# Hybrid diffusion trunk: differential attention first beside the other projections, softmax division of A and B at the output, out-projection in two halves of four k-tiles

## Chip, core and metric

One core of a Trainium2 chip runs the whole inference step, two layers. The metric is the device time of the kernel in microseconds; smaller is better. TensorE (PE) does the matmuls, VectorE (DVE), ScalarE (ACT) and GpSimd (POOL) the rest, and SyncE (SP) and POOL issue the transfers. Each engine takes its instructions from a queue in a fixed order.

## What is computed

There are 128 context tokens and 1024 latent tokens of width 1024, and 256 cached tokens. Each of the two layers is

```python
h = adaln(x, g_attn, shift, scale)                    # modulated RMSNorm
qa, ka, va, qb, kb, vb, qc, kc, vc = split_qkv(h, w_in)   # one projection, 18 blocks of 128 columns
oa = neighborhood_attn(qa, ka, va, cache, rpb)        # A: 4 heads x 64, keys near in the 2-D grid + cached ones, bias
ob = window_attn(qb, kb, vb, cache, sink)             # B: 8 q heads, 2 kv heads, window 128, sink
oc = diff_attn(qc, kc, vc, lam, subln_g)              # C: 4 heads, softmax1 - lam * softmax2 over all keys
x = x + gate * (concat(oa, ob, oc) @ w_out)
h = adaln(x, g_ffn, ...)
x = x + gate * conv_ffn(h)                            # 1024 -> 2 x 2816 -> 1024, width-3 convolution between
```

Every q and k head is RMS-normalised (B and C with a rotary embedding). A softmax row is `exp(s - max) / sum`; in B the sum also holds the sink. The new keys and values of the context tokens are outputs too.

## The kernel before

The tokens lie along the free axis, 1156 columns with padding, in three chunks of some 386. A product of two f32 matrices is three matmuls in fp32r on high and low parts (`gemm`, L480), so that a projection block (`inproj`, L491) is three chunks of 24 matmuls. A block of q or k goes on, for each chunk: ACT squares and copies it out of PSUM, PE sums over the head with a matmul by ones (L515), `rsqrt` follows with Ln and Exp on ACT (L433, L434), one step on DVE (L435) and one on POOL (L436); then POOL scales (L517), DVE finishes (L518), for B and C the rotary embedding runs on DVE and POOL (L525 to L528), and ACT and POOL write the high and low parts `hl` (L551, L552), which SP stores to DRAM as `d`. An attention head loads them again as q and k on POOL's queue (`loadq64` L597, `loadk64` L607; L674 and L678 for C). V, the bias, the caches and the weights come by SP's queue.

An attention block computes scores (L657, L706 for C), DVE adds mask or bias and takes the row's maximum, ACT takes Exp with the row's sum (L660), DVE divides (L853 for A, L797 for B; for C POOL at L715 and DVE at L716 combine the two softmaxes), and `tpv` (L633) transposes P on PE, four tiles to a PSUM bank of the two `tb` banks (L643), ACT copies a bank to `pt` (L645), and PE multiplies by V (L648). After each bank of transposes comes its PV.

The order within a layer is that of the string PLAN (L52), whose steps are projection blocks (`A:4+2`), attention heads (`a:0`, `b:0` for a kv head with two pairs of q heads) and the opening and closing of pools (`fA`, `xA`):

```python
PLAN = "A:4+2 A:0 A:5+3 A:1 mF fA a:0 a:1 a:2 a:3 xA B:11 B:10 B:6 B:7 fB b:0 B:8 B:9 b:1 xB C:16 C:17 C:14 C:15 C:12 C:13"
```

This is program order. A list scheduler then places the instructions into the queues by what is ready in its own model of time, earlier code first; so A attention runs beside the projections that stand behind it, B attention beside C's projections, and C attention (`attnC`, L662) beside `outproj_ab` (L272), the six k-tiles of the out-projection whose heads are A and B, with the O of these read back from DRAM (`odr`). In layer 0 six pieces of the next modulation (`mod_piece`) lie there too. The last two k-tiles (C's) come with the residual and the norm of the FFN. A pool that is opened where another was closed gets its memory, and what is loaded there waits for the last readers.

Of the kernel before, what the change touches and what calls it, by code (L numbers as in the profile page):

```python
# [1078 lines left out]
```

## Time and profile before

| | us |
|---|---|
| median of three runs | 3502.01 (3489.72 to 3503.1) |
| the profiled execution | 3498.61 |
| its span, first to last instruction | 3496.8 |
| PE busy | 3313.9 (95%) |
| DVE busy | 2205.8 (63%) |
| ACT busy | 1524.2 (44%) |
| POOL busy | 1024.6 (29%) |
| mean granted clock of PE, share of full speed | 0.974 |

A layer is some 1000 us of norm, projections, attention and out-projection, in layer 0 from 0 to 1000 and in layer 1 from 1775 to 2700, and some 700 to 800 us of FFN behind it, in which PE is never idle. In layer 0, A attention lies at 150 to 350, B attention at 350 to 605, C attention at 605 to 885. A page's busy time is the sum over the span; the windows of a stage say more of that stage. The granted clock is given as a share of 2.4 GHz.

### The profile page before, as it was taken

The numbers are of one execution on the slowest core, as the hardware profiler recorded it, in microseconds if no ns is written. First come the engines' busy times: TensorE is split into PE (matmuls) and PEld (weight loads), VectorE is DVE, ScalarE is ACT, GpSimd is POOL, SyncE is SP. The second block draws the span as 40 slices with busy tenths as digits, with TensorE's granted clock in tenths as the row PEclk, the third lists the DMA queues.
The fourth block names the chain that finished last, engine by engine and source line by source line (L and its number), as shares of the span: only waits on it lengthen the run. The fifth ranks groups of instructions, "written<-read, shape, count | busy, mean of one in ns | idle before, by whom it ended". The sixth has DMA issues, their size and how long they took to land. (4 is left out here: it accounts for less than half of the span.)

```text
span 3496.8 us, 53582 instructions
## 1 busy us (share of the span) xinstructions
PE 3313.9 (95%) x20014; PEld 2985.7 (85%) x20014; DVE 2205.8 (63%) x5070; ACT 1524.2 (44%) x2941; POOL 1024.6 (29%) x1034
## 2 busy tenths in 40 slices
PE   6989998998899999999999999989888999999999
PEld 4967875865799999999989788768667999999999
DVE  5356677676775875687473557787867544544445
ACT  4555666556522222222245556666664322232222
POOL 5444252432711011101164443423335110111110
PEclk9999998998999999999999999989989999999999
DMA  5765554562122322222137654633401111111112
GB/s 198 204 157 146 129 129 156 139 188 54 40 65 62 91 83 64 72 91 77 43 128 192 168 149 120 142 115 106 102 17 37 34 44 44 43 37 46 46 39 95
DMA packets 197300, 340.23 MB, mean 97 GB/s; under 512 B 59408, under 2 KB 134816, under 8 KB 196656
## 3 DMA queue, kind: packets, MB, share of 16 engines
q1 hardware_dynamic: 183376, 288.89, 27.0%
q0 software_dynamic: 13664, 47.91, 6.7%
q8 instruction: 159, 2.61, 0.3%
q14 instruction: 101, 0.83, 0.1%
HBM read 282.20 MB, written 58.73 MB: 97 GB/s over the span
## 5 line engine op out<-in xcount | busy, mean ns | idle before, releaser
L488 PE MATMUL mm<-h,whl 128*128 128x386 f32 (+2 forms) x4512 | 882.3, 345 | 11.0 <-DVE t L435 4.5
L488 PEld LDWEIGHTS mm<-h,whl 128*128 128x128 f32 x4512 | 802.5, 190 | 29.2 <-DVE t L435 6.4
L488 PE MATMUL s<-h,whl 128*128 128x386 f32 (+2 forms) x4128 | 781.4, 343 | 19.2 <-ACT h L475 9.3
L488 PEld LDWEIGHTS s<-h,whl 128*128 128x128 f32 x4128 | 737.9, 190 | 35.7 <-ACT h L475 14.0
L370 POOL TENSOR_TENSOR whl<-wraw,whl 128x1024 fp32r<-128x1024 f32 (+1 forms) x96 | 227.1, 2367 | 1347.0 <-ACT whl L369 1260.9
L369 ACT ACTIVATE whl<-wraw 128x1024 fp32r<-128x1024 f32 (+1 forms) x246 | 234.9, 957 | 480.5 <-PE s L488 264.7
L660 ACT ACTIVATE P<-P,nm 128x641 f32<-128x641 f32 (+4 forms) x360 | 345.0, 959 | 131.5 <-DVE nm L708 44.3
L488 PE MATMUL s<-ah,whl 128*128 128x384 f32 (+1 forms) x1272 | 356.5, 341 | 2.7 <-DVE x L870 2.6
L643 PE MATMUL tb<-ident,P 128*128 128x128 f32 x1600 | 285.8, 295 | 17.6 <-DVE P L716 12.6
L645 ACT ACTIVATE pt<-tb 128x512 f32<-128x512 f32 (+2 forms) x456 | 235.9, 541 | 152.4 <-PE tb L643 150.7
L648 PE MATMUL pv<-pt,v 128*64 128x128 f32 x3200 | 272.6, 291 | 23.3 <-ACT pt L645 22.0
L648 PEld LDWEIGHTS pv<-pt,v 128*64 128x64 f32 x3200 | 173.1, 139 | 121.8 <-ACT pt L645 52.0
L643 PEld LDWEIGHTS tb<-ident,P 128*128 128x128 f32 x1600 | 189.0, 146 | 98.4 <-issue 63.4
L870 DVE SCALAR_TENSOR_TENSOR x<-s,m,x 128x257 f32<-128x257 f32 (+3 forms) x347 | 169.8, 514 | 145.7 <-PE s L488 145.4
L488 PE MATMUL mm<-ah,whl 128*128 128x384 f32 (+1 forms) x840 | 243.2, 341 | 0.4 <-DVE x L870 0.3
L488 PEld LDWEIGHTS s<-ah,whl 128*128 128x128 f32 x1272 | 234.3, 189 | 7.0 <-PE mm L488 2.8
L657 PE MATMUL s<-k,q 128*128 128x256 f32 (+2 forms) x816 | 184.5, 339 | 36.4 <-DMA q<-d 16.2
L488 PE MATMUL mm<-o,whl 128*128 128x384 f32 (+1 forms) x984 | 211.6, 353 | 5.0 <-ACT o L628 1.7
L488 PE MATMUL s<-al,whl 128*128 128x384 f32 (+1 forms) x636 | 215.8, 339 | 0.0
L870 DVE SCALAR_TENSOR_TENSOR x<-mm,m,x 128x257 f32<-128x257 f32 (+3 forms) x293 | 144.1, 514 | 113.5 <-PE mm L488 113.1
L370 DVE TENSOR_TENSOR whl<-wraw,whl 128x768 fp32r<-128x768 f32 (+1 forms) x150 | 166.4, 1110 | 46.7 <-ACT whl L369 46.1
L488 PEld LDWEIGHTS mm<-o,whl 128*128 128x128 f32 x984 | 179.3, 196 | 15.1 <-ACT whl L369 3.5
(195 smaller groups left out, 4942.0 us busy)
## 6 DMA issues: line engine op xcount, KB each, us to landing
wraw<-wup SPq DMA_DIRECT2D x88, 512.0 KB
mraw<-wmod SPq DMA_DIRECT2D x48, 512.0 KB
mraw<-wmv SPq DMA_DIRECT2D x96, 256.0 KB
wraw<-wdn SPq DMA_DIRECT2D x64, 384.0 KB
k<-d POOLq DMA_DIRECT2D x80, 288.5 KB, 6.8
wraw<-win SPq DMA_DIRECT2D x36, 512.0 KB
wraw<-woab SPq DMA_DIRECT2D x48, 384.0 KB
rope<-rope SPq DMA_DIRECT2D x36, 386.0 KB
```

What stands on the lines that cost most here:

```text
L369: nc.scalar.activation(hl[:, 0, :n], raw[:, :n], AF.Copy)
L370: lo_eng.tensor_tensor(hl[:, 1, :n], raw[:, :n], hl[:, 0, :n].bitcast(F32), op=ALU.subtract)
L488: nc.tensor.matmul(ps, w_, r_[:, a:b], start=(i == 0), stop=(i == tot - 1))
L643: nc.tensor.transpose(t[:, 128 * j:128 * j + 128], it[0], self.ident)
L645: nc.scalar.activation(pt[:, :n], t[:, :n], AF.Copy)
L648: nc.tensor.matmul(ps[64 * i:64 * i + 64, :128], V[:, vb], pt[:, 128 * j:128 * j + 128], start=first[i], stop=left[i] == 0)
L657: nc.tensor.matmul(dst, q, view(ks[i]), start=(i == 0), stop=(i == 1))
L660: self.nc.scalar.activation(P[:, :n], P[:, :n], AF.Exp, scale=-1.0, bias=nm, accum_out=sums)
L870: nc.vector.scalar_tensor_tensor(xx, ps[:, s - a:e - a], m[:, col + ob, v:v + 1], xx, op0=ALU.mult, op1=ALU.add)
```

## The change

PLAN begins with C: its blocks 14, 12, 16, then heads 0 and 1, the other C blocks, heads 2 and 3, with all A and B blocks behind them in program order. After that come A attention in a pool of its own, B attention with the out-projection of A's and C's four k-tiles (`outproj_first`) behind it, and the four k-tiles of B, whose O stays in SBUF, with the residual and norm. Weights of the out-projection are loaded once for t = 0 and once for t = 1 and 2 together. For the latent blocks of A and B, `softrow` writes the row's sum into a column of `sums`; after each half of the blocks a reciprocal is taken, PE turns the columns into rows (`rows_over`), and one DVE instruction multiplies 512 columns of O by them. `tpv` first writes all transposes and copies, then all PV. The sink copy moves from DVE to POOL, and buffer counts change. Lines of the kernel after are 10 to 40 higher: L488 is L498, L515 is L525, L517 is L527, L436 is L446, L526 is L536, L552 is L562, L597 is L607, L607 is L617, L643 is L651, L648 is L660, L657 is L681, L706 is L730.

```diff
-PLAN = "A:4+2 A:0 A:5+3 A:1 mF fA a:0 a:1 a:2 a:3 xA B:11 B:10 B:6 B:7 fB b:0 B:8 B:9 b:1 xB C:16 C:17 C:14 C:15 C:12 C:13"
+PLAN = "C:14+12 C:16 fC c:0 c:1 C:15+13 C:17 c:2 c:3 mF A:4+2 A:0 A:5+3 A:1 B:11 B:10 B:6 B:7 mP B:8 B:9 xC"
 QY = {"A": "p", "B": "p", "C": "p"}
 NM0, NMC = 8, 3
 MODF = (3, 4)
-NT_I, NQG_I, NHL_I, NR_I = 7, 5, 3, 2
-NQ_A, NK_A, NV_A, NB_A, NP_A, NT_A = 2, 2, 2, 7, 3, 3
-NQ_B, NK_B, NV_B, NP_B, NT_B = 3, 2, 1, 5, 4
-NQ_C, NK_C, NV_C, NP_C, NT_C = 2, 3, 1, 7, 3
+NT_I, NQG_I, NHL_I, NR_I = 6, 5, 2, 2
+NQ_A, NK_A, NV_A, NB_A, NP_A, NT_A = 2, 4, 2, 7, 5, 6
+NQ_B, NK_B, NV_B, NP_B, NT_B = 3, 2, 1, 6, 6
+NQ_C, NK_C, NV_C, NP_C, NT_C = 2, 2, 1, 5, 5
...
-OT = {"A": 0, "B": 2, "C": 6}
-INORDER = ["C", "B", "A"]
+OT = {"A": 0, "C": 2, "B": 4}
...
-                self.odr = self.dram.tile([6, 128, W], F32, name=f"odr{l}")
+                self.odr = self.dram.tile([4, 128, W], F32, name=f"odr{l}")
...
                     elif step[0] == "f":
-                        ap, aps = self.open(step[1], "right")
+                        cp, cs = self.open(step[1], "right")
                     elif step[0] == "x":
-                        aps.close()
-                    elif step[0] == "a":
-                        self.attnA(ap, int(step[2:]))
-                    elif step[0] == "b":
-                        self.attnB(ap, int(step[2:]))
+                        cs.close()
+                    elif step[0] == "c":
+                        self.attnC(cp, int(step[2:]))
...
-                cp, cs = self.open("C")
-                self.attnC(cp)
                 xp, xs = self.open("x", "right")
                 x = xp.tile([128, KT, XW], F32, name="x")
                 for t in range(3):
                     self.loadx(x, t)
+                obp, obs = self.open("OB")
+                self.mmtags = TAGS["F"]
+                ap, aps = self.open("A", "right")
+                for h in range(4):
+                    self.attnA(ap, h)
+                aps.close()
                 ab, abs_ = self.open("oab")
                 if l == 0:
                     for j in (4, 5):
                         self.mod_piece(l, j, ab, self.mm(), NMC)
-                self.outproj_ab(x, ab)
+                ap, aps = self.open("B", "right")
+                self.op = obp
+                for kv in range(2):
+                    self.attnB(ap, kv)
+                aps.close()
+                self.outproj_first(x, ab)
...
-                ow = [self.finO(ohp, t, {k: self.O[k][:, OCHUNK[t][0]:OCHUNK[t][1]] for k in (6, 7)}, 12) for t in range(3)]
+                ow = [self.finO(ohp, t, {k: self.O[k][:, OCHUNK[t][0]:OCHUNK[t][1]] for k in range(4, 8)}, 24) for t in range(3)]
                 for ts in ((0,), (1, 2)):
                     for ob in range(KT):
-                        if ob % 4 == 0:
-                            whl = self.wload(a["woc"][l, ob // 4], nc.vector)
+                        if ob % 2 == 0:
+                            whl = self.wload(a["wo"][l, 1, ob // 2], nc.vector)
                         for t in ts:
                             c0, c1 = OCHUNK[t]
                             ps = self.mm()
-                            self.gemm(ps[:, :c1 - c0], whl, (6, 7), (2 * (ob % 4), 2 * (ob % 4) + 1), ow[t], 0, c1 - c0)
+                            self.gemm(ps[:, :c1 - c0], whl, range(4, 8), [4 * (ob % 2) + i for i in range(4)], ow[t], 0, c1 - c0)
...
-    def outproj_ab(self, x, pool):
+    def outproj_first(self, x, pool):
         nc, a, l = self.nc, self.a, self.l
-        for t in range(3):
-            c0, c1 = OCHUNK[t]
-            n = c1 - c0
-            raw = pool.tile([128, 6, 388], F32, name="oraw", bufs=1)
-            nc.sync.dma_start(raw[:, :, :n], self.odr[:, :, c0:c1].rearrange("k p w -> p k w"))
-            ow = self.finO(pool, t, {k: raw[:, k, :n] for k in range(6)}, 14)
+        for ts in ((0,), (1, 2)):
+            ow = {}
+            for t in ts:
+                c0, c1 = OCHUNK[t]
+                raw = pool.tile([128, 4, 388], F32, name="oraw", bufs=1)
+                nc.sync.dma_start(raw[:, :, :c1 - c0], self.odr[:, :, c0:c1].rearrange("k p w -> p k w"))
+                ow[t] = self.finO(pool, t, {k: raw[:, k, :c1 - c0] for k in range(4)}, 16)
             for ob in range(KT):
-                whl = self.wload(a["woab"][l, ob], nc.vector if (t, ob) > (0, 3) else nc.gpsimd)
-                ps = self.mm()
-                self.gemm(ps[:, :n], whl, range(6), None, ow, 0, n)
-                self.addx(x, ob, ps, c0, c1, 16)
+                if ob % 2 == 0:
+                    whl = self.wload(a["wo"][l, 0, ob // 2], nc.vector)
+                for t in ts:
+                    c0, c1 = OCHUNK[t]
+                    ps = self.mm()
+                    self.gemm(ps[:, :c1 - c0], whl, range(4), [4 * (ob % 2) + i for i in range(4)], ow[t], 0, c1 - c0)
...
-        O = self.op.tile([128, W], F32, name="O", bufs=2)
+        O = self.op.tile([128, W], F32, name="O", bufs=2 if kt < 4 else 4)
...
-        ps = self.bank("pv")
-        left = [sum(it[2] == i for it in items) for i in range(2)]
-        first = [True, True]
+        pts = []
         for g in range(0, len(items), 4):
             its = items[g:g + 4]
             n = 128 * len(its)
@@ -643,14 +651,30 @@
                 nc.tensor.transpose(t[:, 128 * j:128 * j + 128], it[0], self.ident)
             pt = ap.tile([128, 512], F32, name="pt", bufs=bufs)
             nc.scalar.activation(pt[:, :n], t[:, :n], AF.Copy)
-            for j, (_, vb, i) in enumerate(its):
-                left[i] -= 1
-                nc.tensor.matmul(ps[64 * i:64 * i + 64, :128], V[:, vb], pt[:, 128 * j:128 * j + 128],
-                                 start=first[i], stop=left[i] == 0)
-                first[i] = False
+            pts.append(pt)
+        ps = self.bank("pv")
+        left = [sum(it[2] == i for it in items) for i in range(2)]
+        first = [True, True]
+        for g, (_, vb, i) in enumerate(items):
+            left[i] -= 1
+            nc.tensor.matmul(ps[64 * i:64 * i + 64, :128], V[:, vb], pts[g // 4][:, 128 * (g % 4):128 * (g % 4) + 128],
+                             start=first[i], stop=left[i] == 0)
+            first[i] = False
         for dst, p0, p1, view in outs:
             nc.scalar.activation(dst, view(ps[p0:p1, :128]), AF.Copy)
 
+    def rows_over(self, r, n):
+
+        t = self.tb()
+        for u in range(4):
+            o = t[:, 128 * u:128 * u + 128]
+            if n == 1:
+                self.nc.tensor.transpose(o, bcast(r[:, u:u + 1], [[0, 128]]), self.ident)
+            else:
+                for i in range(2):
+                    self.nc.tensor.matmul(o[64 * i:64 * i + 64], bcast(r[:, u, i:i + 1], [[0, 64]]), self.ident, start=True, stop=True)
+        return t
...
-                        nc.vector.tensor_copy(P[:, n:n + 1], sk)
+                        nc.gpsimd.tensor_copy(P[:, n:n + 1], sk)
...
-                        self.softrow(P, n + 1, last, ss)
-                        nc.vector.reciprocal(ss, ss)
-                        nc.vector.tensor_scalar(P[:, :n], P[:, :n], ss, None, op0=ALU.mult)
+                        if qb is None:
+                            self.softrow(P, n + 1, last, ss)
+                            nc.vector.reciprocal(ss, ss)
+                            nc.vector.tensor_scalar(P[:, :n], P[:, :n], ss, None, op0=ALU.mult)
+                        else:
+                            self.softrow(P, n + 1, last, sums[:, qb, i:i + 1])
                         Ps.append(P)
                     qo = C0 if qb is None else L0 + 128 * qb
                     self.tpv(ap, [(Ps[i][:, 128 * k:128 * k + 128], kb, i) for k, kb in enumerate(kbs) for i in range(2)], V, NT_B,
                              [(O[:, qo:qo + 128], 0, 128, lambda z: z)])
-                nc.sync.dma_start(self.odr[OT["B"] + h0 // 2], O)
+                    if qb in (3, 7):
+                        half = sums[:, qb - 3:qb + 1]
+                        nc.vector.reciprocal(half, half)
+                        R = self.rows_over(half, 2)
+                        oo = O[:, L0 + 512 * (qb // 4):L0 + 512 * (qb // 4) + 512]
+                        nc.vector.tensor_tensor(oo, oo, R, op=ALU.mult)
...
-                    self.softrow(P, n, nm[:, 1:2], ss)
-                    nc.vector.reciprocal(ss, ss)
-                    nc.vector.tensor_scalar(P[:, :n], P[:, :n], ss, None, op0=ALU.mult)
+                    if cb is None:
+                        self.softrow(P, n, nm[:, 1:2], ss)
...
+                if cb % 2 == 1:
+                    half = sums[:, 2 * cb - 2:2 * cb + 2]
+                    nc.vector.reciprocal(half, half)
+                    R = self.rows_over(half, 1)[rows]
+                    oo = O[rows, L0:L0 + T].rearrange("p (r b c) -> p b r c", r=ROWS, c=16)[:, cb - 1:cb + 1]
+                    nc.vector.tensor_tensor(oo, oo, R.rearrange("p (b r c) -> p b r c", b=2, c=16), op=ALU.mult)
```

How this moves instructions, at three places of layer 0. In each row the count of equal instructions stands at the end. First, PE's queue at the start of A attention, where L488 (after: L498) are projection matmuls, L515 (L525) the ones-matmul of a chunk, L657 (L681) scores, L643 transposes of P. Before:

```order
L488 MATMUL s<-h,whl 128x384 x22
L488 MATMUL s<-h,whl 128x386 x9
L515 MATMUL mm<-t,ones_86 128x386
L488 MATMUL s<-h,whl 128x386 x13
L657 MATMUL s<-k,q 128x128 x2
L488 MATMUL mm<-h,whl 128x386 x19
L515 MATMUL s<-t,ones_86 128x384
L488 MATMUL mm<-h,whl 128x386
L657 MATMUL s<-k,q 128x384 x2
```

and after:

```order
L525 MATMUL mm<-t,ones_86 128x386
L498 MATMUL mm<-h,whl 128x384 x29
L525 MATMUL s<-t,ones_86 128x386
L498 MATMUL s<-h,whl 128x386 x24
L525 MATMUL mm<-t,ones_86 128x384
L525 MATMUL s<-t,ones_86 128x386 x2
L525 MATMUL mm<-t,ones_86 128x384
L525 MATMUL s<-t,ones_86 128x386
L681 MATMUL s<-k,q 128x128
L681 MATMUL s<-k,q 128x384
L681 MATMUL s<-k,q 128x256 x2
```

The scores of A's first head stood between projection matmuls; now they stand behind the last of them, with five ones-matmuls in a row ahead.

Second, POOL's queue at the same place; d_0 is A's q of block 0, d_2 its k. Before:

```order
L517 TENSOR_TENSOR qg<-qg,t 128x386
L436 TENSOR_TENSOR t<-t 128x386
L547 TENSOR_TENSOR hl<-qg,hl 128x6x4x16 x2
L517 TENSOR_TENSOR qg<-qg,t 128x386
L436 TENSOR_TENSOR t<-t 128x386
L597 DMA q<-d_0_800 64x1152 x4
L552 TENSOR_TENSOR hl<-qg,hl 128x386
L517 TENSOR_TENSOR qg<-qg,t 128x384
L436 TENSOR_TENSOR t<-t 128x384
```

and after, the end of B's last block and the first loads of A:

```order
L527 TENSOR_TENSOR qg<-qg,t 128x384
L446 TENSOR_TENSOR t<-t 128x384
L536 TENSOR_TENSOR t<-t,rope 128x384
L562 TENSOR_TENSOR hl<-qg,hl 128x384
L527 TENSOR_TENSOR qg<-qg,t 128x386
L446 TENSOR_TENSOR t<-t 128x386
L536 TENSOR_TENSOR t<-t,rope 128x386
L562 TENSOR_TENSOR hl<-qg,hl 128x386
L607 DMA q<-d_0_3757 64x1152 x2
L617 DMA k<-d_2_3553 64x1154 x4
L607 DMA q<-d_0_3757 64x1152 x2
L617 DMA k<-d_2_3553 64x1154 x4
```

The loads of A's q and k stood between POOL's work on chunks; now they stand behind the last chunk's.

Third, PE's queue at the start of C attention, where L706 (after: L730) are scores and L586 turns the context's V. Before:

```order
L643 MATMUL tb<-ident,P 128x128 x4
L657 MATMUL s<-k,q 128x256 x2
L706 MATMUL s<-k,q 128x128 x2
L643 MATMUL tb<-ident,P 128x128 x2
L648 MATMUL pv<-pt,v 64x128 x8
L643 MATMUL tb<-ident,P 128x128 x4
L706 MATMUL s<-k,q 128x512 x2
L648 MATMUL pv<-pt,v 64x128 x2
L643 MATMUL tb<-ident,P 128x128 x4
```

and after:

```order
L498 MATMUL s<-h,whl 128x386 x22
L525 MATMUL tb<-t,ones_88 128x386
L498 MATMUL mm<-h,whl 128x386 x24
L525 MATMUL tb<-t,ones_88 128x386
L586 MATMUL pv<-ident,qg 128x128 x3
L586 MATMUL mm<-ident,qg 128x128 x3
L586 MATMUL s<-ident,qg 128x128 x3
L730 MATMUL s<-k,q 128x128 x2
L730 MATMUL s<-k,q 128x512 x4
L730 MATMUL s<-k,q 128x256 x2
L730 MATMUL s<-k,q 128x512 x2
```

The first scores of C stood between B's scores, transposes and PV; now they stand behind the ones-matmul of C's last q chunk and the nine transposes of V, with no other work between.

## Rows read from the trace of the kernel before

**Rows 1.** The page's first part: busy us of each engine, share, instructions.

```profile
PE 3313.9 (95%) x20014; PEld 2985.7 (85%) x20014; DVE 2205.8 (63%) x5070; ACT 1524.2 (44%) x2941; POOL 1024.6 (29%) x1034
```

**Rows 2.** Windows: stretch, length, busy PE PEld DVE ACT POOL (instructions), clock, DMA, GB/s.

```profile
175.00:350.00 175.00, 157.55 (x1036) 130.68 (x1035) 100.20 (x279) 98.02 (x229) 80.18 (x100) 0.98 0.58 152
350.00:490.00 140.00, 136.19 (x990) 118.64 (x989) 96.35 (x318) 87.06 (x205) 54.28 (x61) 0.99 0.50 129
490.00:605.00 115.00, 101.68 (x755) 70.82 (x757) 91.84 (x344) 79.79 (x183) 31.07 (x53) 0.90 0.52 148
605.00:750.00 145.00, 141.68 (x928) 117.96 (x928) 107.15 (x245) 82.61 (x145) 64.59 (x67) 0.98 0.53 141
750.00:885.00 135.00, 115.24 (x740) 70.35 (x740) 89.24 (x246) 81.46 (x150) 36.21 (x37) 0.87 0.36 109
...
1200.00:1300.00 100.00, 100.00 (x571) 100.00 (x570) 63.40 (x123) 23.44 (x36) 14.36 (x6) 1.00 0.23 71
...
1890.00:2085.00 195.00, 183.15 (x1192) 156.75 (x1191) 118.23 (x317) 114.46 (x266) 86.53 (x102) 0.97 0.56 150
2085.00:2225.00 140.00, 136.81 (x999) 120.55 (x998) 93.25 (x303) 84.86 (x198) 55.69 (x70) 1.00 0.54 137
2225.00:2365.00 140.00, 121.41 (x907) 86.88 (x905) 107.39 (x388) 96.24 (x218) 51.49 (x75) 0.92 0.50 132
2365.00:2490.00 125.00, 117.28 (x743) 100.72 (x744) 102.73 (x235) 74.12 (x130) 46.28 (x47) 0.94 0.41 109
2490.00:2600.00 110.00, 88.77 (x611) 61.97 (x610) 82.04 (x215) 72.83 (x133) 33.01 (x34) 0.88 0.14 35
```

**Rows 3.** Waits of PE in 175 to 300: total us, times, longest.

```profile
PE s L657 <- DMA k<-d: 8.1, 4, 4.2
...
PE tb L643 <- DVE P L853: 0.6, 1, 0.6
```

**Rows 4.** Waits of PE in 500 to 590.

```profile
PE s L657 <- DMA q<-d: 7.7, 1, 7.7
```

**Rows 5.** Windows: C's last head alone, layer 0.

```profile
807.00:863.00 56.00, 44.60 (x294) 30.08 (x294) 47.44 (x129) 36.95 (x65) 13.16 (x11) 0.82 0.07 13
```

**Rows 6.** Costliest groups: PV matmuls; behind the bars idle before, by releaser.

```profile
L648 PE MATMUL pv<-pt,v 128*64 128x128 f32 x3200 | 272.6, 291 | 23.3 <-ACT pt L645 22.0
```

**Rows 7.** Groups by shape, DVE: the division, B and A; total us, mean ns.

```profile
L797 DVE TENSOR_SCALAR P<-P,ss 128x640 f32<-128x640 f32 x96 | 60.8, 635 | 1.3
...
L853 DVE TENSOR_SCALAR P<-P,ss 128x640 f32<-128x640 f32 x64 | 47.1, 738 | 1.2
```

**Rows 8.** Timeline of PE: start, us for all, instruction, count.

```profile
522.64 0.89 PE L643 MATMUL tb<-ident,P 128*128 128x128 f32 x6
523.63 1.15 PE L648 MATMUL pv<-pt,v 128*64 128x128 f32 x16
```

**Rows 9.** Groups by shape, POOL: rsqrt's last step; loads of q, issue.

```profile
L436 POOL TENSOR_TENSOR t<-t 128x386 f32<-128x386 f32 x52 | 54.4, 1046 | 4.5 <-DVE t L435 4.4
...
L597 POOL DMA_DIRECT2D q<-d x48 | 25.5, 542 | 9.9 <-DMA k<-d 5.3 <-PE s L657 4.1 <-DMA d<-hl 0.5
```

**Rows 10.** Groups by shape, DVE: a step of the rotary embedding.

```profile
L525 DVE STREAM_SHUFFLE t<-qg 128x386 f32<-128x386 f32 x36 | 21.4, 593 | 0.0
```

**Rows 11.** Groups by shape, ACT: a step of rsqrt.

```profile
L434 ACT ACTIVATE t<-t 128x386 f32<-128x386 f32 x52 | 27.4, 526 | 0.9
```

**Rows 12.** Timeline of POOL: A's last context k part, then the load waiting for it.

```profile
108.46 0.46 POOL L533 TENSOR_TENSOR hl<-qg,hl 128x128 fp32r<-128x128 f32 x1 [1.97 <-ACT hl L532]
115.22 2.13 POOL L607 DMA_DIRECT2D k<-d  x4 [6.30 <-issue]
```

**Rows 13.** DMA issues: KB each, median us from issue to landing.

```profile
k<-d POOLq DMA_DIRECT2D x80, 288.5 KB, 6.8
...
q<-d POOLq DMA_DIRECT2D x64, 144.5 KB, 5.6
```

**Rows 14.** Timeline of PE where A attention begins, layer 0.

```profile
146.80 1.04 PE L488 MATMUL s<-h,whl 128*128 128x386 f32 x5
147.68 0.33 PE L657 MATMUL s<-k,q 128*128 128x128 f32 x2
```

**Rows 15.** Instructions of line L716: duration ns min/median/max.

```profile
L716 DVE SCALAR_TENSOR_TENSOR P<-P,ss x72: 331/1548/2614, 568.8 to 2580.2; 128x1280 f32<-128x1280 f32 x64, 128x128 f32<-128x128 f32 x8
```

More of the change, by code (lines that the diff above doesn't have):

```diff
@@ L187, in run @@
                             gens = [g for g in gens if next(g, None) is not None]
-                        if step[0] != "A":
+                        if step[0] != "C":
                             self.gate = None
@@ L208, in run @@
                 abs_.close()
-                cs.close()
                 self.mmtags = MM_SOLO
@@ L229, in run @@
                 ohs.close()
+                obs.close()
                 os_.close()
@@ L270, in run @@
             xs.close()
[L272 removed]
+    def outproj_first(self, x, pool):
         nc, a, l = self.nc, self.a, self.l
[L274 to L284 removed]
+        for ts in ((0,), (1, 2)):
[5 more added lines that the diff above has]
+                ow[t] = self.finO(pool, t, {k: raw[:, k, :c1 - c0] for k in range(4)}, 16)
+            for ob in range(KT):
+                if ob % 2 == 0:
[4 more added lines that the diff above has]
+                    self.gemm(ps[:, :c1 - c0], whl, range(4), [4 * (ob % 2) + i for i in range(4)], ow[t], 0, c1 - c0)
+                    self.addx(x, ob, ps, c0, c1, 16)
     def loadx(self, x, t):
@@ L660, in softrow, with attnC @@
         self.nc.scalar.activation(P[:, :n], P[:, :n], AF.Exp, scale=-1.0, bias=nm, accum_out=sums)
-    def attnC(self, ap):
+    def attnC(self, ap, h):
         nc, l = self.nc, self.l
@@ L665, in attnC @@
         lam = self.lam[l]
-        O = V = None
-        for h in range(4):
+        if True:
             blk, rw = h // 2, 64 * (h % 2)
@@ L689, in attnC @@
             if h % 2 == 0:
-                O = self.newO(OT["C"] + h // 2)
+                self.OC = self.newO(OT["C"] + h // 2)
+            O = self.OC
             rows = slice(rw, rw + 64)
@@ L733, in attnC @@
                                 self.subln(ap, O, c0, c1)
+            if h % 2 == 1:
+                nc.sync.dma_start(self.odr[OT["C"] + h // 2], O)
     def subln(self, ap, O, c0, c1):
@@ L761, in attnB @@
                 O = self.newO(OT["B"] + h0 // 2)
+                sums = ap.tile([128, 8, 2], F32, name="sums", bufs=2)
                 for qb in [None] + list(range(8)):
@@ L823, in attnA @@
             rows = slice(64 * (h % 2), 64 * (h % 2) + 64)
+            sums = ap.tile([128, 8], F32, name="sums", bufs=2)
             for cb in [None, 0, 1, 2, 3]:
@@ L850, in attnA @@
                                                        op0=ALU.add, op1=ALU.min, accum_out=nm[:, 1:2])
-                    self.softrow(P, n, nm[:, 1:2], ss)
-                    nc.vector.reciprocal(ss, ss)
-                    nc.vector.tensor_scalar(P[:, :n], P[:, :n], ss, None, op0=ALU.mult)
+                    if cb is None:
+                        self.softrow(P, n, nm[:, 1:2], ss)
+                        nc.vector.reciprocal(ss, ss)
+                        nc.vector.tensor_scalar(P[:, :n], P[:, :n], ss, None, op0=ALU.mult)
+                    else:
+                        self.softrow(P, n, nm[:, 1:2], sums[:, 2 * cb + rg:2 * cb + rg + 1])
                     Ps.append(P)
@@ L1010, in prep @@
     o["win"] = wblocks(f["w_in"], 18).reshape(DEPTH, 18, 128, 1024)
-    wo = wblocks(f["w_out"], 8)
-    o["woab"] = wo[:, :, :, :6].reshape(DEPTH, 8, 128, 768)
-    o["woc"] = wo[:, :, :, 6:].reshape(DEPTH, 2, 4, 128, 256).transpose(0, 1, 3, 2, 4).reshape(DEPTH, 2, 128, 1024)
+    wo = f["w_out"].reshape(DEPTH, 8, 128, 4, 2, 128)[:, [0, 1, 6, 7, 2, 3, 4, 5]].reshape(DEPTH, 2, 4, 128, 4, 2, 128)
+    o["wo"] = wo.transpose(0, 1, 4, 3, 5, 2, 6).reshape(DEPTH, 2, 4, 128, 1024)
     up = wblocks(f["w_up"], 44).reshape(DEPTH, 2, FB, 128, 1024)
```

## Prediction

> **What bounds the kernel now.** I read the page's totals first [rows 1]: PE 3313.9 of 3496.8 us, 95%, DVE 63%, ACT 44%, POOL 29%. By busy time the kernel is a TensorE kernel, so an edit pays only where it shortens PE's own work or PE's waiting. The profiled run took 3498.6 us, 1.8 us more than its span and 3.4 us less than the median of 3502.01; the sum is made against 3498.6 and the 3.4 us are put back at the end.
>
> The Trainium skill, Perfetto Trace Analysis, section Identifying the Most-Contended Engine, says that matmul busy time is a poor measure of how near TensorE is to its limit, and to use weight-load busy. Here weight loads are at 85%, ten points lower [rows 1]; by that reading there is more to win than the 95% says. The sum does not use it.
>
> Second, the stage windows [rows 2]. The dense stretch 1200 to 1300 is the yardstick: PE 100.00 of 100, 571 matmuls, 0.175 us each, granted clock 1.00 (2.4 GHz). For other stretches I call *lost* the length less PE busy times granted clock. Layer 0's attention: 20.6 us (175 to 350, A attention beside projections), 5.2 (350 to 490, B beside projections), 23.5 (490 to 605, B alone), 6.2 (605 to 750, C beside the out-projection) and 34.7 (750 to 885, C alone, clock 0.87); 90.2 together. Layer 1, the same five: 17.3, 3.2, 28.3, 14.8 and 31.9; 95.5. So 185.7 us are all that re-staging can win; the start of a layer and its end keep their shape.
>
> Third, who is waited for. In 175 to 300 PE waits 8.1 us for A's k loads and 0.6 us for the softmax division [rows 3]; in 500 to 590 one wait of 7.7 us for a q load, since PE's queue is in order [rows 4]. So loads, not DVE's division, are what PE feels in A and B. Over the run, PV waits 22.0 us for ACT's copies out of PSUM [rows 6].
>
> **The change part by part.** *Division to the output.* DVE loses 47.1 + 60.8 us of scaling [rows 7], and more in reciprocals and copies. PE hardly waits for these [rows 3], so I count nothing directly; the cover is PE's own work, and the relief shows in the stage losses below. PE gains 64 transposes and 128 matmuls of 64x128, two records each: at the back-to-back prices of 6 transposes in 0.89 us and 16 PV records in 1.15 us [rows 8], 64 x 0.148 + 256 x 0.072 = 28 us. It lies on PE's path: **+28** (20 to 36).
>
> *PV in bursts, deeper buffers.* At best the 22.0 us of [rows 6] go; at worst more transposes wait for their two PSUM banks and nothing is won. **-14**, nearer the good end because pt now has 6 buffers for the 3 groups of a block of A or B, and 5 for C's 5.
>
> *The new stages.* c0 and c1 run almost without projection matmuls between: a C head alone lost 56 - 44.6 x 0.82 = 19.4 us [rows 5]. Two heads 39, less what the rest of C's projections fill, 30. c2 and c3 beside the twelve A and B blocks: 12 x 72 matmuls x 0.175 = 151 us, two heads at 37 us of PE, some 225 us; between 3% (350 to 490) and 11% (175 to 350) lost, I take 6%: 13. A attention alone: from nothing to B alone's 20% on some 75 us; 10. B beside the first out-projection, 160 us at 4 to 12%, nearer the low end since B's k, q waits and DVE load shrink: 9. Together 62 a layer, 124, less the 14 above 110: **-75.7** against 185.7.
>
> *Hand-over 1, projections to c0.* Before, the first scores of C stood between B's transposes and PV. Now, by the order's rows, they stand right behind the last C ones-matmul in layer 0 (L525 of after, L515 of before) and nine transposes, 24 projection matmuls (4.2 us) being the only other cover in layer 1. c0's q comes out of that very chunk. Its chain: four POOL steps of 1.05 us [rows 9], three of DVE at 0.59 [rows 10] and three of ACT at 0.53 [rows 11] are 7.6 us; the write's landing is 6.3 us by the one place where POOL sat ahead of a load of rows just written [rows 12]; 7 issues of 0.54 us [rows 9], and 5.6 us to landing [rows 13]: 23 us. Less 1.3 and 5.5 us of cover: 22 + 18 = **+40** (15 to 65; not below nothing, since the waits are all true dependences).
>
> *Hand-over 2, projections to a0.* The largest term. Before, A's loads were issued while projections ran, and the first A score took no idle time at all: 147.68, inside a run of projection matmuls [rows 14]. Now pool A opens where C's pool was closed, and a0's six first q and k loads stand behind all POOL work of B8 and B9; on PE five ones-matmuls in a row follow the last 24 projection matmuls, then the a0 scores (the order's rows at the start of A attention). All five chunks' POOL work comes behind those ones-matmuls: 4 instructions each, 4.2 us [rows 9]. POOL runs one chunk to its end before the next, so that three DVE steps and one of ACT between them are not hidden: 6.5 us. Five chunks 21 to 33 us, first Ln and Exp 1.1, six issues 3.3, landing of k 6.8 [rows 9 to 11, 13]: 32 to 44 us, and no PE work in the queue. Both layers have the same order. Middle, 38: **+76**. V's and the bias's loads (SP's queue) wait for the same pool and are no longer than this.
>
> *Hand-over 3, A to B.* Pool B takes A's memory: b0's q waits for a3's last PV and its k for a3's last scores. Four issues and 6.8 us to landing, 9 us, part of it under mod work in layer 0: 8 each, **+16** (6 to 24). The nearest row is the 7.7 us q wait [rows 4].
>
> *At nothing.* The sink copies, moved to POOL, have one column each: POOL is at 31.07 of 115 in B alone [rows 2]. If that cover failed, the next q issues queue behind a copy that waits for its P buffer; that is inside hand-over 3's range. Out-projection: as many matmuls as before, 24 fewer weight loads, hidden in 605 to 750, where PE is at 141.68 of 145. Odr now holds four k-tiles and B's O stays in SBUF: less traffic, not on the path.
>
> Sum: 3498.6 - 75.7 + 28 + 40 + 76 + 16 = 3582.9; with the 3.4 us, 3586. I forecast **3585**. Its own range: stages +/-30, hand-overs 15 + 64 + 6 to 65 + 88 + 24: 3525 to 3640.
>
> **The rivals.** *Stages run at PE's pace (faster).* With 108 us and more off DVE, and bursts, no engine paces c2, c3, A or B, c0 and c1 lose as little as 605 to 750 did, and the hand-overs are at the low ends of their chains (20, 64, 10). For: 2085 to 2225 lost only 3.2 of 140. Against: C's scaling did not move, and c0, c1 have little beside them. Stages lose 5 a layer: 3498.6 - 175.7 + 28 + 94 = 3445, with the 3.4 us 3448. It decides once the stages lose less than 25 a layer (under 3485).
>
> *Half of that (no difference).* Stages lose 30 a layer, hand-overs low: 3498.6 - 125.7 + 28 + 94 + 3.4 = 3498.
>
> *DVE and POOL block each other (slower still).* c2 and c3 now run beside projections, whose POOL instructions fill the gaps. L716 spans 1548 ns at the median and 2614 at most [rows 15]: 32 of these for c2 and c3 in two layers, 1.07 us each, 34 us if PE follows DVE: 3619. The Trainium skill, SBUF — State Buffer, section Who interferes with whom, has a rule for it: a DVE instruction with two SBUF inputs and a GpSimd one that reads SBUF exclude each other for a whole instruction. The spread of L716 agrees with it; the median says it is not the rule here.
>
> *The waits are not there.* That the loads overtake is excluded by POOL's order and true waits; that the scheduler's queue leaves PE other work there is excluded by PE's order. I give it no chance of its own.
>
> **How the numbers follow.** Forecast 0.57; blocking on top 0.11; no difference 0.16; faster 0.16. Slower 0.68. 0.5%, 17.5 us, is about what a measurement of this kernel can tell from no change: faster is under 3484.5, slower above 3519.5. The range for 8 in 10 is 3475 to 3640: about half of the faster case (0.09) and the far end of blocking or of all hand-overs (0.08) lie outside.
>
> **What would show it.** Right: PE idle for 30 us or more ahead of the first A score in each layer, put down to q or k loads, with POOL working through five chunks during it; some 20 us ahead of c0's first score; a granted clock below 0.9 in those slices; DVE's busy time down by 100 us or more; A's stage at 70 us or more. Wrong: an a0 gap under 15 us, which would say that POOL was never behind; or losses inside the stages under 25 us a layer, which the division and the bursts would have earned. Either by itself moves the time by 40 to 75 us.

## Result and the profile after

3747.73 us after (3741.44 to 3747.98) against 3496.11 us before (3489.72 to 3503.1; median of four runs, one more than in the table of the time before): ratio 1.0715, 95% interval 1.0685 to 1.0744, 252 us slower. The forecast was 3585, with a range up to 3640: the sign was right, the size about a third of what came.

The first line is the page's totals of the kernel after, in the form of [rows 1]; the others are windows of its two layers, with the columns of [rows 2].

```profile
PE 3358.6 (90%) x20334; PEld 3018.0 (81%) x20334; DVE 2102.8 (56%) x4590; ACT 1524.1 (41%) x2917; POOL 1042.1 (28%) x1170
...
0.00:148.00 148.00, 87.21 (x382) 60.75 (x382) 66.85 (x141) 52.98 (x105) 86.47 (x110) 0.84 0.58 182
148.00:240.00 92.00, 71.22 (x375) 45.59 (x375) 65.75 (x191) 51.46 (x91) 25.13 (x29) 0.72 0.16 33
240.00:340.00 100.00, 82.71 (x482) 69.31 (x482) 51.38 (x110) 48.26 (x90) 38.89 (x41) 0.91 0.25 71
340.00:526.00 186.00, 177.11 (x1126) 152.86 (x1126) 123.24 (x294) 117.76 (x222) 90.46 (x91) 0.98 0.42 112
526.00:645.00 119.00, 68.73 (x364) 56.42 (x363) 52.40 (x97) 42.68 (x86) 67.89 (x87) 0.81 0.55 166
645.00:767.00 122.00, 93.74 (x707) 65.57 (x707) 46.80 (x176) 65.78 (x169) 19.26 (x42) 0.85 0.78 185
767.00:994.00 227.00, 226.21 (x1851) 181.77 (x1850) 108.98 (x353) 132.03 (x300) 37.59 (x99) 1.00 0.36 107
...
1913.00:2011.00 98.00, 59.17 (x271) 47.96 (x269) 52.03 (x82) 33.69 (x66) 62.63 (x63) 0.87 0.56 166
2011.00:2100.00 89.00, 67.70 (x361) 42.85 (x363) 65.45 (x189) 50.07 (x89) 24.90 (x29) 0.72 0.17 34
2100.00:2200.00 100.00, 81.22 (x476) 66.36 (x473) 48.72 (x110) 48.52 (x90) 34.00 (x34) 0.86 0.22 65
2200.00:2404.00 204.00, 187.33 (x1177) 163.18 (x1175) 132.33 (x308) 121.21 (x232) 97.89 (x102) 0.97 0.40 112
2404.00:2518.00 114.00, 64.13 (x336) 53.20 (x335) 47.57 (x87) 39.92 (x79) 60.07 (x81) 0.79 0.54 162
2518.00:2628.00 110.00, 83.78 (x663) 60.69 (x663) 44.21 (x164) 63.31 (x163) 18.27 (x40) 0.87 0.75 167
```

Taken as lost time (length less PE busy times clock), layer 0 gives: 75 us up to c0's first score, 41 and 25 for c0 and c1, 12 for c2 and c3, 63 up to a0's first score, 42 for A attention and the way to B, 1 for B beside the first out-projection. Before, the same reading of [rows 2] gave 90 for all attention stages. This reading is too large where a stretch holds long idle time, since the low clock of the idle time pulls the mean clock of the whole stretch down. Summed over windows of 1 us (busy time times the clock of that window), the same stretches lose 71, 41, 25, 11, 53, 37 and 1 us, and before 87. Summed like this over the whole runs, the 243 us between the two profiled executions (spans 3739.6 and 3496.8) are 198 us more idle time of PE, 25 us more that PE's work took because of a lower clock, and 20 us more work.

DVE has 103 us less work, and the kernel is slower all the same: PE's busy share fell from 95% to 90%. The FFN behind takes about as long as before.

PE's timeline ahead of A's first score (start, us, instruction; in brackets idle before and its releaser), then POOL's at the same time, then DVE's where A's work begins, then windows of these slices:

```profile
598.69 1.19 PE L525 MATMUL s<-t,ones 128*128 128x386 f32 x2 [2.79 <-ACT qg L523]
605.98 1.65 PE L525 MATMUL s<-t,ones 128*128 128x386 f32 x2 [6.09 <-ACT qg L523]
612.73 1.65 PE L525 MATMUL mm<-t,ones 128*128 128x384 f32 x2 [5.10 <-ACT qg L523]
619.49 1.66 PE L525 MATMUL s<-t,ones 128*128 128x386 f32 x2 [5.11 <-ACT qg L523]
644.77 0.87 PE L681 MATMUL s<-k,q 128*128 128x128 f32 x2 [23.62 <-DMA k<-d]
...
656.79 1.53 PE L681 MATMUL s<-k,q 128*128 128x256 f32 x4 [7.67 <-DVE nm L884]
```

```profile
618.66 0.99 POOL L527 TENSOR_TENSOR qg<-qg,t 128x384 f32<-128x384 f32 x1
...
625.38 1.00 POOL L527 TENSOR_TENSOR qg<-qg,t 128x386 f32<-128x386 f32 x1
626.34 1.00 POOL L446 TENSOR_TENSOR t<-t 128x386 f32<-128x386 f32 x1
628.69 1.19 POOL L536 TENSOR_TENSOR t<-t,rope 128x386 f32<-128x386 f32 x1 [1.35 <-issue]
631.11 1.00 POOL L562 TENSOR_TENSOR hl<-qg,hl 128x386 fp32r<-128x386 f32 x1 [1.23 <-ACT hl L561]
632.05 1.09 POOL L607 DMA_DIRECT2D q<-d  x2
```

```profile
656.11 0.62 DVE L884 CUSTOM_DVE_ANT_0 P<-s,bias,bigt 128x384 f32<-128x384 f32 x1 [8.05 <-DMA bias<-bias]
```

```profile
600.00:620.00 20.00, 3.81 (x5) 1.50 (x6) 8.45 (x18) 7.11 (x15) 12.18 (x13) 0.50 0.41 133
620.00:645.00 25.00, 1.38 (x3) 0.26 (x2) 5.07 (x11) 2.04 (x4) 12.64 (x19) 0.50 0.65 134
645.00:660.00 15.00, 6.89 (x19) 4.46 (x20) 3.92 (x17) 2.66 (x8) 1.48 (x3) 0.50 1.23 253
```

This is the forecast's second hand-over much as it was drawn: five ones-matmuls, POOL going through one chunk after another at 6.7 us (625.38 less 618.66), A's loads behind the last one. Three things were not drawn. The ones-matmuls did not run off at once: from the second on they waited for ACT's step on their chunk, the last three some 7 us apart. After A's first scores PE stood for another 7.67 us, because DVE waited for A's bias. And the clock: it fell to 0.50, the lower of its two levels (1.2 of 2.4 GHz), with PE almost idle, and stayed there for the first 15 us of A's work.

### The profile page after: what moved, and what is told of

Read it like the earlier page. It is cut to its first block, busy times and chain, and to the rows that moved or that the text cites. A ratio compares the mean times of both kernels' runs of the same rounds, so it can differ in the third digit from the quotient of the medians.

```text
span 3739.6 us, 54135 instructions
## 1 busy us (share of the span) xinstructions
PE 3358.6 (90%) x20334; PEld 3018.0 (81%) x20334; DVE 2102.8 (56%) x4590; ACT 1524.1 (41%) x2917; POOL 1042.1 (28%) x1170
## 5 line engine op out<-in xcount | busy, mean ns | idle before, releaser
L498 PE MATMUL mm<-h,whl 128*128 128x386 f32 (+2 forms) x4344 | 852.3, 346 | 30.9 <-DVE t L445 14.3
L498 PE MATMUL s<-h,whl 128*128 128x386 f32 (+2 forms) x4296 | 808.4, 343 | 17.0 <-ACT h L485 4.6
L498 PEld LDWEIGHTS mm<-h,whl 128*128 128x128 f32 x4344 | 776.7, 191 | 58.1 <-DVE t L445 20.3
L498 PEld LDWEIGHTS s<-h,whl 128*128 128x128 f32 x4296 | 766.7, 190 | 35.0 <-ACT h L485 8.9
L380 POOL TENSOR_TENSOR whl<-wraw,whl 128x1024 fp32r<-128x1024 f32 x88 | 211.3, 2401 | 1351.3 <-ACT whl L379 1265.3
L684 ACT ACTIVATE P<-P,nm 128x1280 f32<-128x1280 f32 (+4 forms) x360 | 345.3, 960 | 237.9 <-DVE nm L732 97.5
L379 ACT ACTIVATE whl<-wraw 128x1024 fp32r<-128x1024 f32 (+1 forms) x222 | 219.9, 992 | 475.2 <-PE s L498 280.6
L498 PE MATMUL s<-ah,whl 128*128 128x384 f32 (+1 forms) x1272 | 356.6, 341 | 2.8 <-DVE x L916 2.6
L651 PE MATMUL tb<-ident,P 128*128 128x128 f32 x1600 | 283.6, 298 | 42.7 <-DVE P L740 31.8
L651 PEld LDWEIGHTS tb<-ident,P 128*128 128x128 f32 x1600 | 193.9, 149 | 111.5 <-issue 43.7
L660 PE MATMUL pv<-pt,v 128*64 128x128 f32 x3200 | 268.0, 290 | 1.3 <-ACT P L684 0.6
L916 DVE SCALAR_TENSOR_TENSOR x<-s,m,x 128x257 f32<-128x257 f32 (+3 forms) x347 | 169.9, 513 | 155.8 <-PE s L498 155.5
L681 PE MATMUL s<-k,q 128*128 128x256 f32 (+2 forms) x816 | 183.5, 342 | 71.9 <-DMA k<-d 47.6
L498 PE MATMUL mm<-ah,whl 128*128 128x384 f32 (+1 forms) x840 | 243.3, 341 | 0.4 <-DVE x L916 0.3
L730 PE MATMUL s<-k,q 128*128 128x512 f32 (+2 forms) x400 | 168.7, 467 | 83.5 <-DMA q<-d 51.2
L660 PEld LDWEIGHTS pv<-pt,v 128*64 128x64 f32 x3200 | 174.9, 139 | 80.7 <-issue 56.1
L498 PEld LDWEIGHTS s<-ah,whl 128*128 128x128 f32 x1272 | 234.4, 189 | 7.0 <-PE mm L498 2.8
L498 PE MATMUL s<-al,whl 128*128 128x384 f32 (+1 forms) x636 | 215.9, 339 | 0.0
L681 PEld LDWEIGHTS s<-k,q 128*128 128x128 f32 x816 | 129.5, 200 | 95.8 <-issue 65.7
L730 PEld LDWEIGHTS s<-k,q 128*128 128x128 f32 x400 | 81.3, 215 | 132.5 <-DMA q<-d 50.2
```

The source lines that it names most:

```text
L379: nc.scalar.activation(hl[:, 0, :n], raw[:, :n], AF.Copy)
L380: lo_eng.tensor_tensor(hl[:, 1, :n], raw[:, :n], hl[:, 0, :n].bitcast(F32), op=ALU.subtract)
L498: nc.tensor.matmul(ps, w_, r_[:, a:b], start=(i == 0), stop=(i == tot - 1))
L651: nc.tensor.transpose(t[:, 128 * j:128 * j + 128], it[0], self.ident)
L660: nc.tensor.matmul(ps[64 * i:64 * i + 64, :128], V[:, vb], pts[g // 4][:, 128 * (g % 4):128 * (g % 4) + 128], start=first[i], stop=left[i] ...
L681: nc.tensor.matmul(dst, q, view(ks[i]), start=(i == 0), stop=(i == 1))
```

## Experiments

Times stand beside runs of the kernel before on the same chip (3492 to 3497 us); where two runs on different chips are compared, up to 5 us of the difference can come from that. Line numbers in a view are those of its own run.

**One part alone in the old order.** `e1_div`: attnA and attnB of after (sink copy on DVE) in the kernel before.

> The kernel before with one part of the change: the softmax division of A and B at the output. Theory 1 (the loss lies in the hand-overs of the new stages): PE gains 28 us of work and DVE loses about 100 us that PE hardly waits for, so 3500 to 3525 us. Rival 2 (the division itself costs, PE or DVE waiting for the transposed sums): over 3540. Rival 3 (DVE was what paced A and B): under 3485.

3491.46 us, ratio 0.9991 (0.9981 to 1.0). Its totals, to be read beside [rows 1]:

```profile
PE 3329.5 (96%) x20334; PEld 3002.7 (86%) x20334; DVE 2092.2 (60%) x4750; ACT 1532.8 (44%) x2941; POOL 1016.4 (29%) x1034
```

DVE is 114 us less busy, PE 16 us more, and the time stays within 4 us: in none of the three ranges, so all three theories miss. It can be two effects that cancel. PE's idle time (span less busy) fell from 182.9 to 155.5 us; whether DVE's relief gave that back, and PE's added work took it again, one run with both cannot tell. `e2_burst` and `e6_burst7` take the new `tpv`:

```diff
-NQ_C, NK_C, NV_C, NP_C, NT_C = 2, 3, 1, 7, 3
+NQ_C, NK_C, NV_C, NP_C, NT_C = 2, 3, 1, 6, 5   # e2_burst; 7, 5 in e6_burst7
```

> The kernel before with PV in bursts alone (pt buffers of C 3 to 5, P buffers of C 7 to 6). Theory 1: between -14 us and nothing, 3480 to 3500 us, and PE's wait of PV for ACT's copies falls from 22 us to under 10. Rival 2 (bursts hold the two banks of the transposes and starve PE): over 3510.

> The kernel before with PV in bursts, P buffers of C left at 7 (pt 5). Theory 1 (bursts themselves cost the 50 us of the run with 6 P buffers, since 20 transposes of C go through two banks with no PV to fill the waits for ACT): 3530 to 3555 us. Rival 2 (one P buffer less costs it): 3485 to 3505 us.

3545.7 us (1.0147, 1.013 to 1.0163) and 3506.11 us (1.0038, 1.0025 to 1.0051). Bursts with their buffers cost 14 us, one P buffer less 37 to 40 more: rival 2 of `e6_burst7`, but for 1 us of its range. PE's waits of PV for ACT's copies, over the whole run of `e6_burst7`, to be read beside [rows 6], and its wait for modulation weights in 560 to 960 (1.3 us before):

```profile
PE pv L650 <- ACT pt L643: 3.8, 6, 1.1
```

```profile
PE mm L384 <- DMA mraw<-wmod: 19.5, 3, 13.7
```

The wait that the bursts were for went from 22.0 to 3.8 us, and another came in its place; whether the bursts or their two more `pt` buffers brought that one was not tried apart.

**C's buffers.** `e7_buf5` gives the kernel before C's buffers of after (2, 2, 1, 5, 5), `e13_k2` only the two k buffers (2, 2, 1, 7, 3).

> The kernel before with C's buffers of after (k 2 instead of 3, P 5 instead of 7, pt 5), PV not in bursts. Theory 1 (buffers don't pace C): 3490 to 3505 us. Rival 2 (with 5 P buffers a pair's scores, which need 4, wait for the transposes of the pair ahead): 3530 to 3580 us.

> The kernel before with C's k buffers 3 to 2 alone. Of the 64 us that C's buffers of after cost in the kernel before, theory 1 gives k the smaller part (idle time before scores put down to k rose from 2.4 to 22.9 us): 3505 to 3525 us. Rival 2 (all of it is k): 3540 or more. Rival 3 (all of it is P): under 3500.

3556.89 us (1.0174, 1.0154 to 1.0194) and 3501.78 us (1.0007, 0.9997 to 1.0017). Two P buffers less, with pt at 5, cost some 55 to 60 us (rival 2 of `e7_buf5`); I had not priced them. The k buffer, between the ranges of theory 1 and rival 3, is worth nothing that can be told, though its wait is plain; the first line is `e13_k2`'s over the run, the others `e7_buf5`'s in 560 to 960 (C of layer 0), where before has 5.3 us for the second:

```profile
PE s L706 <- DMA k<-d: 21.8, 7, 5.0
```

```profile
PE tb L643 <- DVE P L716: 13.7, 8, 2.7
PE s L706 <- DMA k<-d: 9.0, 2, 5.0
```

**The new order.** `e3_stage` is after with the old `tpv` and the division on P.

> The kernel after without the bursts and with the division back on P: the new stages, the out-projection in halves, the sink copies on POOL and the new buffer counts alone. Theory 1 (the stages lose the time): 3700 to 3740 us, nearly all of the loss. Rival 2 (bursts or the division lose it in the new stages): under 3620.

3721.47 us (1.0653, 1.0632 to 1.0674): nearly the whole loss is the order's and its buffers', as theory 1 said; with bursts and division the kernel after is 26 us slower than this. `e4_afill` opens A ahead of B's blocks, `e5_call` puts all of C's blocks ahead of c0, `e10_both` does both:

```diff
-C:14+12 C:16 fC c:0 c:1 C:15+13 C:17 c:2 c:3 mF A:... B:11 B:10 B:6 B:7 mP B:8 B:9 xC
+C:14+12 C:16 fC c:0 c:1 C:15+13 C:17 c:2 c:3 mF A:... xC fA a:0 a:1 a:2 a:3 B:11 B:10 B:6 B:7 B:8 B:9 xA   # e4_afill
+C:14+12 C:16 C:15+13 C:17 fC c:0 c:1 c:2 c:3 mF A:... B:11 B:10 B:6 B:7 mP B:8 B:9 xC                       # e5_call
```

> The kernel after with A attention opened as soon as C's heads are done, beside B's projection blocks, instead of behind them (k buffers of A 4 to 2, pt 6 to 5, so that the pool fits). Theory 1 (PE idles some 55 us a layer behind the last projection because A's loads stand behind POOL's five last chunks, and its clock is then low): that gap goes, 3610 to 3640 us, and no PE wait over 12 us ahead of A's first score. Rival 2 (the gap is the reload of the pool's memory and moves along with A): 3700 or more, with a wait of 20 us or more for k or q still there.

> The kernel after with all five C blocks ahead of head c0, so that three more blocks (38 us of matmuls) stand between c0's q chain and its first scores, and A's blocks fill c0 and c1. Theory 1 (c0's q comes late and then c0 and c1 find no matmuls beside them): the 25 us waits for q go, and c0 and c1 lose less; 3680 to 3715 us. Rival 2 (c0 and c1 are paced by their P buffers and DVE, and the filling is only used up earlier): 3735 or more.

> The kernel after with both remedies: all C blocks ahead of c0, and A attention beside B's blocks (k buffers of A 2, pt 5). Theory 1 (the two waits are apart): the gains add, 3600 to 3635 us. Rival 2 (both draw on the same 151 us of A and B projections as filling): 3650 or more.

3667.12 us (1.0497, 1.0476 to 1.0518), 3651.59 us (1.0452, 1.0429 to 1.0476) and 3593.24 us (1.0285, 1.026 to 1.0311). The first gives back 81 us, less than expected: the wait ahead of a0 is 1.08 us, but a wait of PE for k on POOL came up (18.2 us at most in layer 0, 35.4 in all) further on. The time lies between theory 1 and rival 2. The second gives back 96, more than expected. Together 154 of 177: nearly additive. The windows show where `e5_call` won; first after's, then its own:

```profile
0.00:150.00 150.00, 88.39 (x385) 61.63 (x385) 67.55 (x145) 53.47 (x107) 86.47 (x110) 0.84 0.58 180
150.00:250.00 100.00, 77.19 (x406) 49.06 (x406) 73.30 (x213) 58.26 (x102) 27.89 (x32) 0.74 0.15 31
250.00:350.00 100.00, 82.36 (x478) 71.18 (x474) 43.70 (x88) 43.12 (x83) 39.03 (x43) 0.89 0.35 94
```

```profile
0.00:150.00 150.00, 116.09 (x540) 90.84 (x541) 70.02 (x144) 58.06 (x113) 84.28 (x104) 0.92 0.55 177
150.00:250.00 100.00, 81.95 (x425) 66.50 (x424) 62.59 (x157) 52.13 (x102) 47.10 (x46) 0.83 0.40 111
250.00:350.00 100.00, 95.85 (x625) 82.47 (x623) 67.16 (x156) 67.70 (x131) 51.77 (x55) 0.98 0.40 106
```

PE had 155 more matmul records by 150, at a clock of 0.92 instead of 0.84, and c1's stretch was filled: by the mean clock 6 us lost instead of 27, and from 150 to 350 together 38 instead of 70.

**Buffers and bursts in the mended order.** `e11_k3` and `e12_p6` start from `e10_both`, take C out of the bursts (pt 3, qg 4) and give C k 3 or P 6. `e18_noburst` is `e12_p6` with no bursts in A and B, and their buffers as before.

> The run with both remedies (all C blocks ahead of c0, A beside B's blocks; 3593 us), with C's k buffers 2 to 3; to make room C's PV is not in bursts and pt of C 5 to 3, qg 5 to 4. Theory 1 (with two k buffers a head's k is loaded only after the head ahead has read its last): waits for k ahead of C's scores nearly go, 3545 to 3570 us. Rival 2 (P buffers are it, or DVE paces C there): 3580 or more.

> The same with C's P buffers 5 to 6 instead of k 2 to 3 (C's PV not in bursts, pt of C 3, qg 4). Theory 1 (a pair's scores need 4 P buffers, and with 5 they wait for the pair ahead): 3545 to 3575 us. Rival 2 (k buffers are it): 3580 or more.

> The run with both remedies and C's P buffers at 6 (3573 us), with no bursts in A and B either, and A's and B's P and pt buffers as before (A 3 and 3, B 5 and 4). Theory 1 (bursts and the buffers that they ask for cost 19 to 50 us wherever they stand): 3525 to 3555 us. Rival 2 (they cost only in the order of before, where projections lie beside A and B): 3565 or more.

3611.62 us (1.0328, 1.0306 to 1.0349), 3573.48 us (1.0219, 1.0198 to 1.0239) and 3623.43 us (1.0365, 1.0335 to 1.0395). A P buffer instead of a k buffer: 38 us, theory 1 of `e12_p6` and rival 2 of `e11_k3`. Against `e10_both`, which keeps C's bursts with their `pt` and `qg` buffers, the one is 20 us faster and the other 18 slower. But theory 1 of `e18_noburst` falls: here bursts and buffers in A and B earn 50 us. Which of the two earns it was not tried apart; `e3_stage`, which has the buffers and no bursts (nor the division), was faster than the kernel after. In 550 to 850 `e12_p6` loses 70 us by the mean clock, `e18_noburst` 94, spread over A's and B's blocks, which run with little beside them.

**Toward a better one.** `e14_best` is `e1_div` with C's k at 4 and P at 8; `e16_abburst` adds bursts in A and B alone, `e17_abbuf` more P and pt buffers for these.

> The kernel before with the division at the output (3491 us) and more buffers for C: k 3 to 4, P 7 to 8. Theory 1 (C alone is paced by its buffers still): 3450 to 3480 us. Rival 2 (7 and 3 were enough, and DVE paces a C head): 3482 to 3500 us.

> The run with division at the output and C's k and P buffers at 4 and 8 (3489 us), with PV in bursts for A and B alone. In the run with bursts everywhere the stretches of A and B lost less than before (350 to 550: 5.6 us instead of 22.1) and those of C more. Theory 1 (bursts pay where a block has 3 groups of transposes and projections beside it, and cost where C has 5): 3465 to 3482 us. Rival 2 (what A and B win, C loses behind them, since the same filling is used up): 3485 or more.

> The same with B's P and pt buffers at 6 and 6 (from 5 and 4) and A's at 4 and 4 (from 3 and 3). Theory 1 (a burst holds 3 pt and its P longer, so that the next block waits for them): 10 us or more below the run without. Rival 2 (not): within 6 us of it.

`e14_best`: 3489.0 us, 0.9972 (0.9959 to 0.9985): faster than both kernels, in rival 2's range and not theory 1's, and by less than the 17.5 us that the prediction gives as the least that tells a change. The others lose, `e16_abburst` as its rival 2 said, `e17_abbuf` beyond either theory: 3508.25 us (1.0047, 1.003 to 1.0063) and 3539.9 us (1.0138, 1.0123 to 1.0153). In the last one PE's timeline has one wait, behind B's last work, that is longer than the whole difference to `e16_abburst`:

```profile
581.51 3.14 PE L384 MATMUL mm<-mraw,cvz 128*32 128x512 f32 x8 [35.36 <-DMA mraw<-wmod]
```

In that run a load of modulation weights came into PE's way; that the bigger pools of A and B did it, by their memory, is argued from the order, not tried.

## Why the prediction was right in sign and wrong in size

The mechanism held for the hand-overs: PE idles there for the loads that were named. The step that failed is the size of three terms: c0 and c1, hand-over 2 and hand-over 1. Summed over windows of 1 us, they came to 132, 130 and 71 us in the two layers where 60, 76 and 40 stood: 157 us too little, where the profiled execution is 159 over the sum of 3582.9. The other errors nearly cancel.

*PE work, +28.* `e1_div` shows PE 16 us busier, less than the 28, and no time lost. "On PE's path" is not shown: with DVE's relief in the same run, PE's idle time fell by 27 us, and the two cannot be told apart.

*Bursts, -14.* Nothing was the worst case, and they cost. In the old order they cost 14 us (`e6_burst7`) or 19 (`e16_abburst` against `e14_best`, 24 if each is taken against its own before); in the mended new one, with their buffers, they gave 50. The row they were priced by [rows 6] was right and not enough: its wait fell by 18 us and others rose.

*c2 and c3, B beside the out-projection, A's heads.* 13 and 9 us a layer were forecast for the first two; 12 and 22, and 1 and 5, came. A's four heads from 660 to 740 lose some 5 us of the 10. These steps held, but for c2 and c3 of layer 1.

*c0 and c1, 30 a layer.* 65 and 70 came by the mean clock (the lines 148 to 340 and 2011 to 2200), 66 and 67 in windows of 1 us; this is the largest error. Two steps of it failed. One is "less what the rest of C's projections fill": PE has no projection matmul from 148 until 270, so nothing lay beside c0 and the first part of c1.

```profile
270.53 3.99 PE L498 MATMUL s<-h,whl 128*128 128x386 f32 x21
```

The other is the price, taken from a head of the old order [rows 5] that had 7 P buffers: C with 5 is slower, as `e7_buf5` shows. The change's own line, NP_C 7 to 5, stood in the diff and was read as nothing. In `e5_call`, with the same buffers and projections beside these heads, 150 to 350 loses 38 us instead of 70, so the filling is much of it; how the rest divides is not shown. The clock was 0.72 in c0, and it is here that it costs: of c0's 41 us half are idle time and half work at the lower clock.

*Hand-over 1, 22 and 18.* Waits of 25.0 and 24.0 us for q came, one in each layer. Up to c0's first score 71 us are lost in layer 0 and 42 in layer 1, against 32 and 9 before (windows of 1 us): 38 and 33 more. The first two lines are windows of the kernel before; the others are POOL's and PE's timelines after.

```profile
0.00:148.00 148.00, 120.14 (x593) 94.65 (x594) 63.51 (x126) 68.29 (x136) 84.37 (x109) 0.97 0.69 213
1775.00:1890.00 115.00, 107.53 (x557) 97.39 (x556) 62.64 (x91) 54.05 (x108) 75.57 (x79) 0.99 0.62 181
...
128.24 2.15 POOL L701 DMA_DIRECT2D k<-d  x4 [6.80 <-DMA d<-hl]
...
131.05 0.90 POOL L536 TENSOR_TENSOR t<-t,rope 128x386 f32<-128x386 f32 x1
137.40 0.47 POOL L705 TENSOR_SCALAR kr<-kc,hsel 128x256 fp32r<-128x256 f32 x1 [5.45 <-DMA kc<-kc]
137.85 0.99 POOL L562 TENSOR_TENSOR hl<-qg,hl 128x386 fp32r<-128x386 f32 x1
...
147.91 0.44 PE L730 MATMUL s<-k,q 128*128 128x128 f32 x1 [25.01 <-DMA q<-d]
...
2010.87 0.45 PE L730 MATMUL s<-k,q 128*128 128x128 f32 x1 [24.03 <-DMA q<-d]
```

The members of the chain were right, but POOL's queue was not read to its end: k's loads and the cached keys stand there ahead of the last steps on q's chunk (L536, L562), and POOL waited 6.8 and 5.5 us for them. The 6.3 us for a write's landing was read from a wait that [rows 12] puts down to "issue"; the 6.8 us here, put down to the write, bear it out.

*Hand-over 2, 38 a layer.* The waits are 2.8 + 6.1 + 5.1 + 5.1 + 23.6 = 43 us, at the upper end of 32 to 44: POOL's chunk is 6.7 us, as worked out. The stretch lost 53 us in windows of 1 us (63 by its mean clock), and A's first 15 us another 12: 65, and as much in layer 1. In these 65 us the low clock is 6, since PE had little work while it lasted. The rest is idle time that was not in the sum: 8 us behind A's first scores, where the forecast took the loads of V and the bias to be "no longer than this", and some 8 in short waits earlier in the stretch.

*Hand-over 3, 8.* 14.6 us for modulation weights in layer 0, 5.6 for q and 7.0 for ACT in layer 1, and the last 27 us before 767 at a clock of 0.62. The modulation work that was to cover a part of it brought the wait in layer 0.

*Rivals.* The faster one asked for stage losses under 25 us a layer, the one of no difference for 30; c0 and c1 alone lost 66. "DVE and POOL block each other" was not the loss either: DVE's combining step (L716, after: L740) took 1851 ns in the mean in c2 and c3 of layer 0 and 1551 in c0 and c1, 0.3 us more beside projections and not 1.07, and PE lost 12 us there where 13 were forecast, though 22 in layer 1. The groups of 340 to 526 and of 148 to 340:

```profile
L740 DVE SCALAR_TENSOR_TENSOR P<-P,ss 128x1280 f32<-128x1280 f32 x15 | 27.8, 1851 | 6.3 <-POOL P L739 6.3
L740 DVE SCALAR_TENSOR_TENSOR P<-P,ss 128x1280 f32<-128x1280 f32 x16 | 24.8, 1551 | 11.7 <-POOL P L739 11.7
```

Put together: both hand-over remedies are worth 154 us (`e10_both`), two P buffers some 55 to 60 in the old order, one 20 in the new, net of the loss of C's bursts. Of the 101 us by which `e10_both` is slower than before, the P buffers carry a part that was not tried in full. What else is in it, other than the wait of 18 us a layer between A and B, stays open.

## What to carry to other kernels

Before an order of stages is changed, go through every hand-over: what work is left in the waiting engine's queue, what must end before the first load can be issued, and which engine still has a backlog; and look whether the work that is to fill a stage really lies beside it in the queue. Price the low clock by the work that runs at it and not by the length of the gap: here it was half of c0's loss, but 6 of the 65 us around hand-over 2. A shorter list of buffers is a term of the sum like any other, most of all where one step needs nearly all of them (a pair of C's blocks needs four P). Work taken off an engine that is not the bottleneck need not show in the time: 114 us of DVE's here, with 16 more of PE's, moved it by 4.

## What the runs showed that I had not expected

A wait that is plain in the trace can be free: the k buffer of `e13_k2` added 19 us of waits before C's scores and 4 us of time, within the interval of none. And nearly the same edit can change its sign with the order around it: in A and B, bursts cost 19 us beside projections (51 with more buffers in `e17_abbuf`, 35 of them its one wait for modulation weights) and, with their buffers, gave 50 in the mended new order. The clock of 0.50 held for the whole of 600 to 660, also while PE had begun to work again, and was back at 0.98 in the mean over the next 20 us.
